# One square-root operation for two chunks of the gated recurrence in a two-layer trunk

## The chip, the cores and the metric

The kernel runs on one core of a Trainium2 chip. The metric is device time in microseconds (us) of one execution. Before the change the median of three runs is 1958.04 us (1957.45 to 1959.89). The profile shown here is of one more execution of the same program.

## What is computed

Two layers, each on 2048 rows of width 1024. A layer normalises its input, multiplies it by one wide matrix and splits the product into parts: the input `za` and gate `ga` of a linear recurrence, the latents of an attention, the attention's gate, and the input and gate of a pooling. The three results are gated, joined, multiplied by an output matrix and added to the input. The part that matters here:

```
r   = sigmoid(xa @ w_r + b_r);  i = sigmoid(xa @ w_i + b_i)      # xa = causal conv of za
log_a = -8 * r * softplus(-lam);  a = exp(log_a)
u   = sqrt(-expm1(2*log_a)) * (i * xa)
h_t = a_t * h_(t-1) + u_t                                          # along the sequence
ya  = h * silu(ga)
```

There are 384 recurrence channels (three groups `j` of 128 partitions) and the sequence is cut into four chunks `c` of 512, so a layer has 12 square roots of a 128x512 tile, and the two layers have 24.

## The kernel before, in words

The first part of each layer is a list of product groups `(m, c)`: block `m` of 128 output columns for chunk `c`. A group is 24 matmuls (L403), a little over 5 us, accumulated in one PSUM bank. The list runs over five sets of blocks (`ZSETS`): in the first three sets, for each chunk in turn, come the recurrence input `m = j` (0, 1, 2), the recurrence gate `m = 3 + j`, and two or three other blocks: the attention's gate (15, 16, 17) beside `j = 0`, pooling blocks (11, 13 and 12, 14) beside `j = 1` and `j = 2`. Weights of a block are loaded, squared, scaled and split in two halves just ahead of use: `prep` does it (DMA L216, ACT squares L222, a small matmul L228, DVE scale L185 to L190, ACT high half L231, DVE low half L232), into six slots that are reused, so later blocks can be prepared only when an earlier block has been used for the last time.

When a group's matmuls are issued, its follow-up is started as a Python generator that is stepped once or several groups later (`spawn`, `tick`). `lru_in` is the follow-up of the recurrence input: ACT takes the product out of PSUM (L474), ACT and DVE do the convolution (L476, L478), four product instructions and four tanh follow (L488, L491), then exp and tanh (L492, L493) and four DVE operations (L495 to L498) that leave in slot 1 of the chunk's scratch what the root is taken of (L496). `lru_out` is the follow-up of the gate: ACT tanh into slot 5 (L520), DVE (L521). After an odd chunk, `lru_in` issues the two roots, of the even chunk before and of its own, one after the other (L502 to L504), and then for both chunks `lru_end`: multiply (L512), the scan along the sequence (L513), a copy of its last column (L514), the gating into slot 5 (L515), and `emit_y`: a DMA of slot 5 to memory and a square with accumulation on ACT (L425, L426).

Scratch of a chunk is six slots of 128x512, chosen by `6 * (c % 2) + n`: of the eleven slots of tile `lsa`, slots 0 to 5 belong to even chunks and 6 to 10 to odd ones; the twelfth slot is in `lsb`. Slot 1 of an even chunk is `lsa[:, 1]`, that of an odd chunk `lsa[:, 7]`. The next even chunk writes slot 5 (L520) only when the even chunk before it has sent slot 5 to memory.

The source order is not the order on the engines. When the program is built, a list scheduler with a cost model of its own walks through the instructions by dependence, with source order as priority, and writes a fixed order for each engine's queue; it also places the semaphores. An instruction that becomes ready early and finds its engine free is put ahead of later ones in the source. The loads of ScalarE's function tables (ACT_TABLE_LOAD) are put in ahead of an activation that needs another set of functions than the one before it, and carry that activation's line. At run time each queue is worked through in its fixed order.

Beside this, in the same stretch, the output matrix is read and split (`out_prep`, L890 to L911, with DMAs both ways), and in the first set the next chunk's input is normalised and transposed (`hstage`: squares L340, scaling L351, transposes L356, halves L360 and L361).

Of the kernel before, what the change touches and what calls it, by code (L numbers as in the profile page):

```python
# [13 lines left out]
AF = mybir.ActivationFunctionType  # L14
# [8 lines left out]
C = 512  # L23
# [32 lines left out]
def body(nc, tc, a, ctx):  # L56
# [14 lines left out]
    def PS(tag, name):  # L71
        return psum.tile([128, 512], F32, tag=tag, bufs=BANKS[tag], name=name)
# [14 lines left out]
    tiny = cst.tile([128, 2], F32, name="tiny")  # L87
# [323 lines left out]
    def layer(st):  # L411
# [8 lines left out]
        lsa = mq.tile([128, 11, 528], F32, tag="cqh", name="lsa")  # L420
# [35 lines left out]
        def parted(x):  # L456

            xs = LT("xa", F32R)[:, 0:C], LT("xb", F32R)[:, 0:C]
            for t, h, o in ((xs[0], slice(0, 64), slice(64, 128)), (xs[1], slice(64, 128), slice(0, 64))):
                nc.scalar.activation(t[h], x[h], AF.Copy)  # L460
                nc.vector.tensor_tensor(t[o], x[h], t[h].bitcast(F32), ALU.subtract)
            return xs
# [4 lines left out]
        def scratch(c, n):  # L467
            x = 6 * (c % 2) + n
            return lsa[:, x, 0:C] if x < 11 else lsb[:, x - 11, 0:C]

        def lru_in(j, c, ps, sc):
            za, xa = lsb[:, 1 + c % 2, :], scratch(c, 0)
            nc.vector.tensor_copy(za[:, 0:3], halo[:, j, 0:3])
            nc.scalar.activation(za[:, 3 : 3 + C], ps[:], AF.Copy, scale=sc[:, 2:3])  # L474
            nc.vector.tensor_copy(halo[:, j, 0:3], za[:, C : C + 3])
            nc.scalar.activation(xa, za[:, 0:C], AF.Identity, scale=prm[:, l, j, 0:1], bias=prm[:, l, j, 4:5])  # L476
            for t in range(1, 4):
                nc.vector.scalar_tensor_tensor(  # L478
                    xa, za[:, t : t + C], prm[:, l, j, t : t + 1], xa, ALU.mult, ALU.add
                )  # L480
            xs = parted(xa)
            yield YG
            tr, ti, tt, eh = (scratch(c, n) for n in (1, 2, 3, 4))
            for b in range(2):

                pg = PS("ax", "pg")
                for i in range(2):
                    nc.tensor.matmul(pg[:], gws[j][:, i, b, :], xs[b], start=i == 0, stop=i == 1)  # L488
                for g, t_ in ((0, tr), (1, ti)):
                    h, o = slice(64 * g, 64 * g + 64), slice(64 * b, 64 * b + 64)  # L490
                    nc.scalar.activation(t_[o], pg[h, :], AF.Tanh, scale=0.5, bias=gp[h, l, j, b : b + 1])  # L491
            nc.scalar.activation(eh, tr, AF.Exp, scale=gp[:, l, j, 2:3], bias=gp[:, l, j, 2:3])  # L492
            nc.scalar.activation(tt, tr, AF.Tanh, scale=gp[:, l, j, 3:4], bias=gp[:, l, j, 3:4])  # L493

            nc.vector.scalar_tensor_tensor(eh, eh, 1.0, tt, ALU.add, ALU.mult)  # L495
            nc.vector.scalar_tensor_tensor(tr, eh, 2.0, eh, ALU.subtract, ALU.mult)  # L496
            nc.vector.tensor_scalar(tt, eh, -1.0, 1.0, ALU.mult, ALU.add)
            nc.vector.scalar_tensor_tensor(ti, ti, 1.0, xa, ALU.add, ALU.mult)  # L498
            yield 1
            if c % 2:  # L500

                for x in (c - 1, c):  # L502
                    t = scratch(x, 1)
                    nc.scalar.activation(t, t, AF.Sqrt, scale=-1.0, bias=tiny[:, 0:1])  # L504
                for x in (c - 1, c):
                    lru_end(j, x, sgs[j, x])

# [2 lines left out]
        def lru_end(j, c, sc):  # L510
            tr, ti, tt, hsn, sg = (scratch(c, n) for n in (1, 2, 3, 4, 5))
            nc.vector.scalar_tensor_tensor(ti, tr, 0.5, ti, ALU.mult, ALU.mult)  # L512
            nc.vector.tensor_tensor_scan(hsn, tt, ti, halo[:, j, 3:4], ALU.mult, ALU.add)  # L513
            nc.vector.tensor_copy(halo[:, j, 3:4], hsn[:, C - 1 : C])  # L514
            nc.vector.scalar_tensor_tensor(sg, sg, sc[:, 3:4], hsn, ALU.mult, ALU.mult)  # L515
            emit_y(sg, j, c)
# [409 lines left out]
        for g, (m, c) in enumerate(groups):  # L926
            if g < g1 and (g == 0 or (g + HL) % len(ZSETS[0]) == 0):
                nxt = (g + HL) // len(ZSETS[0]) + (1 if l == 0 else 2)
                if nxt < NC:
                    early_room = [lsb[:, 3 + n, 0:C] for n in range(4)] + [lsa[:, (7 + n) % 11, 0:C] for n in range(10)]  # L930
                    spawn(st["hstage"](nxt, True, early_room if l == 0 and nxt == 1 else None))
            for ev in events.get(g, ()):
                ev()
            for w in begin.get(g, ()):
                spawn(zweight(st, w, late=2))
            if m == "kr":
                krope()
                tick()
                continue
            ps, sc = zgroup(st, m, c, g < g1)  # L940
            if m < 3:
                spawn(lru_in(m, c, ps, sc))
            elif m < 6:
                spawn(lru_out(m - 3, c, ps, sc))
            elif m < 8:
                spawn(latent("k", m - 6, c, ps, sc))
            elif m < 11:
                spawn(latent("q", m - 8, c, ps, sc))
            elif m < 13:
                spawn(pool_in(m - 11, c, ps, sc))  # L950
            elif m < 15:
                spawn(pool_gate(m - 13, c, ps, sc))
            else:
                spawn(attn_gate(m - 15, c, ps, sc))
            tick()
# [425 lines left out]
```

## Time and profile before

| | |
|---|---|
| median of three runs | 1958.04 us |
| the profiled execution, its own time | 1964.85 us |
| its span, first to last instruction | 1962.8 us |
| mean granted TensorE clock | 0.991 |
| busy: TensorE / VectorE / ScalarE / GpSimd | 1890.9 / 1454.6 / 1145.0 / 45.5 us |
| share of the span | 96% / 74% / 58% / 2% |

PE stands for TensorE's matmuls, DVE for VectorE, ACT for ScalarE, POOL for GpSimd and SP for the engine that issues DMAs. Times inside the profile count from the start of the span. The bracket at the end of a timeline line is the time for which the engine stood idle ahead of it, and what ended the wait.

### The profile page before, as it was taken

Reading aid. Unit: us, or ns where it says so; the run is one execution under the profiler, and the core shown is the slowest. Engines: PE = TensorE matmul, PEld = TensorE weight load, DVE = VectorE, ACT = ScalarE, POOL = GpSimd, SP = SyncE. Lnnn points to the kernel's source line nnn. Section 1 sums busy time; section 2 is a strip of 40 time slices with the busy share of each in tenths; the row PEclk is TensorE's granted clock in tenths of the full one; section 3 lists DMA queues with packets and bytes.
Section 4 is the critical chain, followed back from the end, with each engine's and each line's share of the span. In section 5 each row is a group of like instructions: output and inputs, shape, how many; then the busy total and the mean of one; then the engine's idle time right before and its main releaser. Section 6 shows DMA issues by size and latency. Waiting matters only on the chain. (4 is left out here: it accounts for less than half of the span.)

```text
span 1962.8 us, 32908 instructions
## 1 busy us (share of the span) xinstructions
PE 1890.9 (96%) x12352; PEld 980.2 (50%) x12352; DVE 1454.6 (74%) x3345; ACT 1145.0 (58%) x2060; POOL 45.5 (2%) x38
## 2 busy tenths in 40 slices
PE   8999999999889999999999999999999999999998
PEld 4444444444455555555454444444444555555553
DVE  8757788767888787774485568778687977977745
ACT  8767877644355465464286578775434644644641
POOL 0000000010000000000000000001010000000000
PEclk9999999999999999999999999999999999999999
DMA  6313242212453121122751223231134621421443
GB/s 217 111 49 108 82 134 101 62 38 65 103 168 119 44 92 52 37 76 77 245 168 53 75 81 122 100 105 46 49 76 110 192 77 44 154 84 59 158 160 136
DMA packets 125280, 197.74 MB, mean 101 GB/s; under 512 B 18752, under 2 KB 41536, under 8 KB 125120
## 3 DMA queue, kind: packets, MB, share of 16 engines
q1 hardware_dynamic: 125120, 195.64, 31.6%
q8 instruction: 97, 1.59, 0.3%
q14 instruction: 63, 0.52, 0.1%
HBM read 124.59 MB, written 55.26 MB: 92 GB/s over the span
## 5 line engine op out<-in xcount | busy, mean ns | idle before, releaser
L403 PEld LDWEIGHTS <-zw 128*128 128x128 f16 x3456 | 335.9, 99 | 401.3 <-issue 22.0
L1048 ACT ACTIVATE p<-sps,tiny,sig 128x512 f32<-128x512 f32 x480 | 322.0, 710 | 326.2 <-PE sps L1045 174.7
L403 PE MATMUL zps<-hA,zw 128*128 128x512 f16 x1728 | 398.0, 384 | 5.1 <-ACT zw L231 3.9
L403 PE MATMUL zps<-hB,zw 128*128 128x512 f16 x1728 | 382.7, 379 | 0.0
L1122 PE MATMUL ops<-wo,yb 128*128 128x512 f16 x1536 | 370.2, 380 | 6.3 <-DVE xr L1114 4.0
L1049 DVE TENSOR_TENSOR pl<-p 128x1024 f16<-128x1024 f32 x240 | 253.9, 1059 | 127.2 <-ACT p L1048 101.0
L1122 PEld LDWEIGHTS <-yb 128*128 128x128 f16 x1536 | 144.9, 98 | 172.4 <-issue 9.9
L822 DVE TENSOR_REDUCE mx<-pm 128x1 f32<-128x512 f32 x288 | 192.5, 683 | 21.9 <-PE pm L817 21.8
L1043 PE MATMUL sps<-kq 97*128 97x512 f16 x480 | 167.1, 348 | 3.0 <-ACT p L1048 2.9
L1044 PE MATMUL sps<-kq 96*128 96x512 f16 x480 | 166.6, 347 | 0.0
L1045 PE MATMUL sps<-kq 96*128 96x512 f16 x480 | 165.7, 345 | 0.0
L817 PE MATMUL pm<-kq 96*128 96x512 f16 (+3 forms) x496 | 151.0, 345 | 5.6 <-DVE mx L822 2.7
L1062 PE MATMUL av<-zw,p 128*128 128x129 f16 (+1 forms) x1632 | 140.2, 214 | 5.2 <-ACT ar L1012 5.2
L1062 PEld LDWEIGHTS <-p 128*128 128x128 bf16 x1632 | 108.5, 98 | 30.4 <-PE sps L1047 1.1
L824 DVE CUSTOM_DVE_ANT_0 pm<-pm,mkq 128x128 f32<-128x128 f32 (+1 forms) x208 | 101.0, 495 | 12.7 <-PE pm L817 11.8
L1062 PE MATMUL av<-zw,pl 128*128 128x65 f16 x1632 | 92.9, 194 | 1.7 <-DVE pl L1049 1.7
L1062 PEld LDWEIGHTS <-pl 128*128 128x128 f16 x1632 | 75.1, 98 | 12.2 <-DVE pl L1049 8.0
L491 ACT ACTIVATE lsa<-pg,gp 64x512 f32<-64x512 f32 x96 | 65.3, 680 | 12.0 <-PE pg L488 10.4
L1045 PEld LDWEIGHTS <-kq 96*128 96x128 f16 x480 | 47.0, 98 | 43.6 <-issue 1.9
L1043 PEld LDWEIGHTS <-kq 97*128 97x128 f16 x480 | 46.6, 97 | 44.3 <-issue 4.7
L1044 PEld LDWEIGHTS <-kq 96*128 96x128 f16 x480 | 47.2, 98 | 43.1 <-issue 4.8
L1067 PE MATMUL av<-zw,p 128*128 128x64 f16 x336 | 64.8, 193 | 0.0
(300 smaller groups left out, 2604.1 us busy)
## 6 DMA issues: line engine op xcount, KB each, us to landing
xk<-x SPq DMA_DIRECT2D x80, 256.0 KB
raw<-win SPq DMA_DIRECT2D x72, 256.0 KB
raw<-wout SPq DMA_DIRECT2D x64, 256.0 KB
yr<-y SPq DMA_DIRECT2D x64, 256.0 KB
xr<-x SPq DMA_DIRECT2D x56, 256.0 KB
x<-xr SPq DMA_DIRECT2D x56, 256.0 KB
sg<-sg SPq DMA_DIRECT2D x48, 256.0 KB
kq<-pq SPq DMA_DIRECT2D x96, 128.0 KB
```

What stands on the lines that cost most here:

```text
L403: nc.tensor.matmul(ps[:], w[:, i, k, :], st["h"](j, k, c), start=n == 0, stop=n == 3 * KD - 1)
L491: nc.scalar.activation(t_[o], pg[h, :], AF.Tanh, scale=0.5, bias=gp[h, l, j, b : b + 1])
L817: nc.tensor.matmul(pm[:, 0:n], t[0:96, h, 2, q0 : q0 + 128], t[0:96, h, 0, s * C : s * C + n], start=True, stop=True)
L822: nc.vector.tensor_reduce(m, pm[:], AX.X, ALU.max)
L824: nc.vector.tensor_tensor_reduce(out=pm[:, 0:n], in0=pm[:, 0:n], in1=mkq[:, C - n : C], op0=ALU.add, op1=ALU.max, scale=1.0, scalar=-3.0e3 ...
L1043: nc.tensor.matmul(ps[:, o:C], t[0:97, h, 0, ks], t[0:97, h, 2, qs], start=True, stop=False)
L1044: nc.tensor.matmul(ps[:, o:C], t[0:96, h, 0, ks], t[0:96, h, 3, qs], start=False, stop=False)
L1045: nc.tensor.matmul(ps[:, o:C], t[0:96, h, 1, ks], t[0:96, h, 2, qs], start=False, stop=not diag)
L1048: nc.scalar.activation(pw_[:, h, o:C], ps[:, o:C], AF.Exp, scale=sig[:, 4:5], bias=tiny[:, 1:2])
L1049: nc.vector.tensor_tensor(pl[:, :, o:C], pw_[:, :, o:C], ph[:, :, o:C], ALU.subtract)
L1062: nc.tensor.matmul(acc[h][:, c - 64 * lo : c + 65], w, v[:, 64 - 64 * lo : QB], start=first and n == 0 and j == 0, stop=end and n == 1 and ...
L1122: nc.tensor.matmul(ps[:], yb[:, j, k, 128 * (n // 2) : 128 * (n // 2) + 128], wo[n % 2, k][:, i, :], start=m == 0, stop=m == 3 * KD - 1,)
```

## The change

The two roots after an odd chunk become one activation over both chunks' slot 1, a view of `lsa` with a step of six slots. All else is as it was.

```diff
@@ -499,9 +499,8 @@
             yield 1
             if c % 2:
 
-                for x in (c - 1, c):
-                    t = scratch(x, 1)
-                    nc.scalar.activation(t, t, AF.Sqrt, scale=-1.0, bias=tiny[:, 0:1])
+                t = lsa[:, 1:8:6, 0:C]
+                nc.scalar.activation(t, t, AF.Sqrt, scale=-1.0, bias=tiny[:, 0:1])
                 for x in (c - 1, c):
                     lru_end(j, x, sgs[j, x])
```

## Rows read from the trace of the kernel before

**Rows 1.** The page, busy time (us), share of the span, instructions of an engine

```profile
PE 1890.9 (96%) x12352; PEld 980.2 (50%) x12352; DVE 1454.6 (74%) x3345; ACT 1145.0 (58%) x2060; POOL 45.5 (2%) x38
```

**Rows 2.** Windows, six stretches with the recurrence (30 to 360, 1000 to 1320): busy us, summed

```profile
sum 650.00, PE 634.54 PEld 306.31 DVE 472.43 ACT 495.17 POOL 7.71; mean PE 105.76 PEld 51.05 DVE 78.74 ACT 82.53 POOL 1.28
```

**Rows 3.** Line 504 of the kernel: duration ns min/median/max, starts, forms

```profile
L504 ACT ACT_TABLE_LOAD  x24: 1283/1283/1283, 57.5 to 1313.0; - x24
L504 ACT ACTIVATE lsa<-lsa,tiny x24: 721/722/723, 58.8 to 1314.3; 128x512 f32<-128x512 f32 x24
```

**Rows 4.** ACT groups by line and shape: busy us, mean ns, idle before

```profile
L1048 ACT ACTIVATE p<-sps,tiny,sig 128x512 f32<-128x512 f32 x336 | 247.6, 774 | 213.1 <-PE sps L1045 174.7 <-PE sps L1047 33.2 <-DVE pl L1049 3.1
...
L520 ACT ACT_TABLE_LOAD x18 | 23.1, 1283 | 0.3
...
L1048 ACT ACTIVATE p<-sps,tiny,sig 128x128 f32<-128x128 f32 x48 | 19.9, 454 | 37.7 <-PE sps L1047 21.9 <-PE av L1062 10.7 <-DVE ysc L190 3.7
...
L715 ACT ACT_TABLE_LOAD x4 | 5.1, 1283 | 0.1
...
L1048 ACT ACT_TABLE_LOAD x2 | 2.6, 1283 | 0.0
```

**Rows 5.** ACT in order of time (start us, us), around the first chunk's root

```profile
57.54 1.28 ACT L504 ACT_TABLE_LOAD   x1
58.84 0.72 ACT L504 ACTIVATE lsa<-lsa,tiny 128x512 f32<-128x512 f32 x1
...
67.20 1.28 ACT L520 ACT_TABLE_LOAD   x1
```

**Rows 6.** PE in order of time, the longest wait of the first layer's stretches

```profile
259.30 0.61 PE L403 MATMUL zps<-hA,zw 128*128 128x512 f16 x2 [1.92 <-ACT zw L231]
```

**Rows 7.** Windows, 260 to 265: us; busy PE, PEld, DVE, ACT, POOL; granted clock; DMA

```profile
260.00:265.00 5.00, 4.71 (x14) 1.82 (x15) 4.74 (x9) 2.99 (x6) 0.00 (x0) 0.66 0.30 105
```

**Rows 8.** ACT in order of time, ahead of the wait at 259

```profile
254.00 0.72 ACT L907 ACTIVATE wp<-raw,wosc 128x512 f16<-128x512 f32 x1 [3.11 <-DMA wo<-wp]
254.74 1.28 ACT L520 ACT_TABLE_LOAD   x1
256.03 0.69 ACT L520 ACTIVATE lsa<-zps,zsc 128x512 f32<-128x512 f32 x1
...
258.54 1.32 ACT L231 ACTIVATE zw<-raw,zsc 128x512 f16<-128x512 f32 x2
```

**Rows 9.** DVE groups by line, the recurrence's end: busy us, mean ns, idle before

```profile
L513 DVE TENSOR_TENSOR_SCAN lsa<-lsa,halo 128x512 f32<-128x512 f32 x24 | 31.2, 1299 | 0.4
...
L512 DVE SCALAR_TENSOR_TENSOR lsa<-lsa 128x512 f32<-128x512 f32 x24 | 16.5, 688 | 5.0 <-ACT lsa L504 5.0
...
L515 DVE SCALAR_TENSOR_TENSOR lsa<-lsa,zsc 128x512 f32<-128x512 f32 x12 | 8.9, 742 | 0.0
...
L514 DVE COPY halo<-lsa 128x1 f32<-128x1 f32 x24 | 3.6, 149 | 0.2
```

**Rows 10.** DVE in order of time, ahead of the wait at 259

```profile
253.49 0.74 DVE L515 SCALAR_TENSOR_TENSOR lsb<-lsb,zsc,lsa 128x512 f32<-128x512 f32 x1
...
254.82 0.16 DVE L190 TENSOR_SCALAR zsc<-hb 128x2 int32<-128x2 int32 x1
```

**Rows 11.** SP in order of time, DMAs issued ahead of the wait at 259

```profile
249.56 1.10 SPq L911 DMA_DIRECT2D wo<-wp  x2
```

**Rows 12.** PE and ACT in order of time, the wait at 341, behind an even chunk

```profile
341.65 0.50 PE L572 MATMUL pg<-xh,pw 128*128 128x512 f32 x1 [0.88 <-ACT xh L567]
...
340.97 0.63 ACT L567 ACTIVATE xh<-sa 128x512 fp32r<-128x512 f32 x1 [1.22 <-DVE sa L565]
```

**Rows 13.** DVE in order of time, the even chunk's end ahead of the wait at 341

```profile
331.76 0.74 DVE L515 SCALAR_TENSOR_TENSOR lsa<-lsa,zsc 128x512 f32<-128x512 f32 x1
```

**Rows 14.** PE and ACT in order of time, the wait at 106, behind an odd chunk

```profile
106.41 0.41 PE L356 MATMUL ht<-idt,xk 128*128 128x128 f32 x2 [1.50 <-DVE xk L351]
...
93.81 0.63 ACT L426 ACTIVATE junk<-lsb 128x512 bf16<-128x512 f32 x1 [0.92 <-DVE lsb L515]
```

## The prediction, made before the changed kernel was run

> **What bounds the kernel now.** I read the page's busy times first. TensorE is busy for 1890.9 of 1962.8 us, ScalarE for 1145.0 [rows 1]: the matmuls set the time, and work taken from ScalarE counts only where TensorE waits for it. So I next summed the windows of the six stretches in which the recurrence runs. In their 650 us TensorE is busy for 634.54, which leaves 15.5 us of idle time in both layers together, while ScalarE is busy for 495.17, or 76% [rows 2]. 15.5 us is the most that the edit could take out of waits there, however much it saves on ScalarE.
>
> Then line 504 itself. The source has the two roots side by side, so one would expect one table load for a pair. The trace shows 24 loads of 1283 ns at L504, one for each of the 24 roots [rows 3], and 24 loads at the activations that follow and need the other set: 18 at L520, 4 at L715, 2 at L1048 [rows 4]. In order of time the first root runs at 58.84, alone, behind its load at 57.54, and the set is loaded back at 67.20 [rows 5]; two roots side by side would need no load between them, so each of the 24 stands alone. The list scheduler has taken the even chunk's root, and with it that chunk's scan and output, ahead of the odd chunk. One operation over both buffers can't be split that way, so what the edit really does is to tie the even chunk's end to the odd chunk's.
>
> **The change part by part.**
>
> *Table loads.* 12 roots in place of 24, with the tanh and exp of the next chunks still between them, need 12 loads and 12 loads back. Removed: 24 x 1.283 = 30.8 us of ScalarE. The sqrt of rows 5 starts 1.30 us after its load's start, so the row shows no cost beside the load's own 1283 ns. The Trainium skill, in "ScalarE: Activation LUTs", section "What ACT_TABLE_LOAD costs", puts a drain of about 1380 ns beside each load, 2.66 us in all; by that estimate the relief would be 63.8 us. The row disagrees, and the relief lies beside the matmuls in either case; the larger figure would only give more weight to the faster rival below.
>
> *The roots.* 24 x 722 ns = 17.3 us [rows 3] become 12 of twice the size. The trace has no activation of 1024 elements; the exponentials cost (774 - 454) / 384 = 0.833 ns for an element more [rows 4], so one takes 722 + 512 x 0.833 = 1149 ns, and 12 take 13.8 us. The bounds are 722 ns (a free second half) and 1444 (two roots). Removed: 3.5 us. Together ScalarE gives up 34.3 of its 1145.0 us, 3.0%. What hides all of it is the matmul stream, and without that cover it would be 34.3 us.
>
> *What is moved.* The even chunk's L512, L513, L514 and L515, 0.688 + 1.299 + 0.149 + 0.742 = 2.88 us of DVE [rows 9], its y DMA on SP and its square on ACT go later by about a chunk's time, five groups of matmuls, behind the odd chunk's root, which itself ends 0.43 us later. Twelve places (the even chunks) lose this work and twelve (the odd ones) get it twice. No one misses the even y, which is read again only by the output product at the layer's end. The state passed along the scans keeps its order. The even slot 5 is held longer, and that is the new wait: L520 of the chunk after the pair must not write it until the pair's first y has gone out. So I went through the waits of TensorE in the recurrence's stretches and asked on which side each lies.
>
> *Behind an even chunk* there is one wait of note, at 341.65, 0.88 us for L567 on ACT, which waited 1.22 us for DVE's L565 [rows 12]. The even chunk's end is part of DVE's work ahead of it: its L515 is at 331.76 and writes `lsa`, the even buffer [rows 13]. Taking 2.88 us out there covers the wait: -0.9. The second layer repeats the pattern, so twice: -1.8 us, between 0 and -1.8.
>
> *Behind an odd chunk* lies the longest: 1.92 us at 259.30, for the high half of a weight block, L231 [rows 6], and the second layer has it again at the same place. After the first the granted clock is 0.66 over five us, between the two levels 0.5 and 1 (1.2 and 2.4 GHz), behind an engine that had just stood idle [rows 7]: another 5 x 0.34 = 1.7 us. So this place costs about 3.6 us a layer, 7.2 in all. It keeps its loads, because the chunk that has just ended is an odd one, whose L515 at 253.49 writes `lsb` [rows 10]: ACT then waits 3.11 us for a DMA (L907), loads back at 254.74, does L520 at 256.03 and comes to L231 at 258.54 [rows 8]. DVE's scale for that block, L190, is done at 254.98 [rows 10], 3.6 us before L231 starts. The extra DVE work, 2.88 + 0.43 = 3.3 us, just fits into that. But slot 5's release does not: the even y now has the place of the odd one, L515 ending at 254.23 [rows 10], and a DMA of the same size, issued at 249.56 to 250.66 [rows 11], let L907 go at 254.00, 3.3 us after the issue. So L520 could start at 254.3 + 3.3 = 257.6, and not at 256.03. If the queue keeps its order, L231 is 1.6 us later in each layer, +3.2 us; if the scheduler puts L231 ahead of L520, 0 or a gain. I take half, +1.6, because the scheduler also counts DMAs, though by its own durations.
>
> At 106.41 TensorE waited 1.50 us for an input chunk whose squares stand behind the odd chunk's L426 at 93.81 [rows 14]. One more such square is 0.63 us, and waiting for both scans costs at most 2.88. I take +0.4, nearer to the square, because the squares of the input don't depend on the scans and can be put ahead. This is in the first layer alone.
>
> *Sum.* -1.8 + 1.6 + 0.4 = +0.2 us. Bounds: all of the losses and no gain, 3.2 + 2.88 = +6.1; all gains and no loss, -1.8, and -9.0 if the weight wait also goes. The profiled execution took 1964.85 us, its span and 2.05 us around it, 0.35% above the median of the runs shown; that difference is no part of the change, so I carry the sum to the median: 1958.04 + 0.2, which is **1958.2 us**. A measurement of this kernel can tell some 0.2% from no change, 3.9 us, so this is "no difference".
>
> **The rivals.**
>
> *Faster: the weight wait disappears.* A table load and reload fewer in each second chunk, and fewer DVE operations ahead, let the scheduler or the queue bring L231 forward. For it: 7.2 us hang on one ACT instruction in each layer that had its scale ready 3.6 us early [rows 8, 10]; ACT was held by L907 and not by work. Against it: the root at that place is an odd chunk's, whose two loads remain. Time: 1958.0 - 7.2 - 1.8 = 1949. I give 0.27 for over 3.9 us faster; some of the way there (one layer, or the clock alone) is enough.
>
> *Slower: the even buffer holds up ACT.* At the first L520 behind a pair, ACT, which works through its queue in order, waits for the y DMA with L231 behind it. Five pairs of six in a layer have such an L520; it decides where the next weight block has under 1.6 us to spare, which is the place at 259 [rows 6] and its like in the second layer. If both scans also stand ahead of L190, L231 comes 3.3 us later and the clock stays low for as much longer: up to 3.3 + 1.7 = 5.0 us a layer, +10 in two, less the 1.8 gained elsewhere: 1962 to 1966. For it: the 3.3 us that a DMA took here. Against it: behind the other pairs TensorE waits for no weights now, and the scheduler can fill in other work. Of the same kind is a rule of the Trainium skill, "Perfetto Trace Analysis", section "Optimizing Scalar/DVE Operations": where these engines are not saturated but cause bubbles elsewhere, smaller instructions let work be done sooner, so a merger would cost. At 76% ScalarE is such an engine. No row shows yet that a root's size holds anyone up. I give 0.26.
>
> *The edit does not do what it says.* If the merged root still saw two loads and two halves, or if the view with a step of six were taken as everything between slots 1 and 7, more waits would follow. The accesses to the slots in between come before the root or after the chain that needs it anyway, so the price would be under 1 us, and the time 1958. It lies inside "no difference", at 0.05 of its 0.47.
>
> **How the numbers follow.** No difference 0.47, faster 0.27, slower 0.26. For eight times in ten the range leaves out the far end of each rival: it goes down to 1949.5, just short of the loss of both weight waits, and up to 1965.0, one us below the full price of the slower one. The likeliest case alone spans 1954.3 to 1962.1.
>
> **What would show it.** Right: 12 roots of about 1.15 us at L504, 12 loads there and 12 at the lines behind, ScalarE's busy time near 1111 us, two sets of L512 to L515 behind each root, and TensorE's idle time in the stretches still near 15 us. The wait at 341 gone, and the start of L520 behind a pair on the landing of the pair's first y. Wrong, on the fast side: no wait for L231 and a granted clock of 1.00 in its place; on the slow side: that wait above 3 us, or new waits for weights behind other odd chunks. I would be wholly wrong if the roots were still apart in the trace, or if TensorE's busy time itself changed by more than 4 us.

## The result, and the profile after

The changed kernel is slower, by three quarters of a per cent:

| | before | after |
|---|---|---|
| median, 6 runs each (us) | 1958.97 (1954.21 to 1964.08) | 1973.15 (1971.36 to 1984.23) |
| ratio, 95% interval | | 1.0075 [1.0059, 1.0092] |
| the profiled execution, its own time (us) | 1964.85 | 1971.64 |
| its span (us), granted clock | 1962.8, 0.991 | 1969.8, 0.993 |

The two profiled executions are 6.8 us apart and the medians 14.2: the one of before is 5.9 us above its median, the one of after among its fastest. The profile therefore shows about half of the loss. From L504 on, line numbers of after are one less than before's.

The edit did what it says. From the page of after, and from the root's line and the groups of table loads:

```profile
PE 1888.2 (96%) x12352; PEld 979.8 (50%) x12352; DVE 1452.8 (74%) x3345; ACT 1110.3 (56%) x2024; POOL 47.0 (2%) x38
```

```profile
L503 ACT ACT_TABLE_LOAD  x12: 1283/1283/1283, 88.8 to 1322.0; - x12
L503 ACT ACTIVATE lsa<-lsa,tiny x12: 1147/1148/1150, 90.3 to 1323.3; 128x1024 f32<-128x1024 f32 x12
```

```profile
L519 ACT ACT_TABLE_LOAD x8 | 10.3, 1283 | 0.7 <-DMA y<-lsa 0.5
...
L714 ACT ACT_TABLE_LOAD x2 | 2.6, 1283 | 0.0
...
L1047 ACT ACT_TABLE_LOAD x2 | 2.6, 1283 | 0.0
```

Twelve roots of 1148 ns, 12 loads for them and 12 back: against [rows 3, 4], 24 loads and 34.7 us of ScalarE are gone. Nothing of that reached the end. The windows of the six stretches, summed as in [rows 2]:

```profile
sum 650.00, PE 628.65 PEld 304.43 DVE 467.98 ACT 456.27 POOL 8.64; mean PE 104.78 PEld 50.74 DVE 78.00 ACT 76.05 POOL 1.44
```

ScalarE is busy for 38.9 us less there, 4.2 more than it lost in all, because the windows stand still and the slower kernel has a little less of its work inside them. TensorE stands idle in them for 650 - 628.65 = 21.4 us instead of 15.5. Which waits grew is in the sums of TensorE's waits by the line that ended them (us in total, times, longest). First the kernel before, then after:

```profile
PE zps L403 <- ACT zw L231: 3.9, 2, 2.0
...
PE pn L245 <- DVE zsc L185: 2.8, 2, 1.4
...
PE pg L572 <- ACT xh L567: 1.8, 2, 0.9
...
PE pp L228 <- DVE wosc L185: 1.7, 2, 0.9
...
PE zps L403 <- DVE zw L232: 0.8, 2, 0.4
```

```profile
PE pp L228 <- DVE wosc L185: 5.7, 2, 2.8
...
PE pn L245 <- DVE zsc L185: 5.1, 2, 3.1
...
PE zps L403 <- DVE zw L232: 2.9, 2, 1.6
...
PE pg L571 <- ACT lsa L491: 2.8, 2, 1.5
...
PE pg L571 <- ACT xh L566: 2.3, 2, 1.7
```

Each is there twice, once in a layer. The wait for ScalarE's high half L231 is gone (-3.9) and one for DVE's low half L232 has come (+2.1). Three waits that are not for a weight block's halves grew: for DVE to read a small product out of its bank, `wosc` (+4.0) and `pn` (+2.3), and for the pooling's product at L571 (+3.3). These five make +7.8 us. All of TensorE's waits together went from 58.5 to 67.5 us, +9.0, while its busy time fell by 2.7 [rows 1]; the span grew by 7.0.

**The place at 259**, where the prediction had looked hardest. PE, ACT and DVE of after in order of time; [rows 6, 8, 10] are the same place before (L190 is the weight block's scale, L511 and L512 of after are the end's multiply and scan):

```profile
261.84 5.24 PE L403 MATMUL zps<-hA,zw 128*128 128x512 f16 x22 [1.59 <-DVE zw L232]
...
251.13 1.28 ACT L503 ACT_TABLE_LOAD   x1
252.43 1.15 ACT L503 ACTIVATE lsa<-lsa,tiny 128x1024 f32<-128x1024 f32 x1
...
254.19 1.32 ACT L231 ACTIVATE zw<-raw,zsc 128x512 f16<-128x512 f32 x2
...
262.55 1.28 ACT L519 ACT_TABLE_LOAD   x1
...
253.24 0.17 DVE L190 TENSOR_SCALAR zsc<-hb 128x2 int32<-128x2 int32 x1
253.61 1.93 DVE L511 SCALAR_TENSOR_TENSOR lsa<-lsa 128x512 f32<-128x512 f32 x2 [0.20 <-ACT lsa L503]
...
256.12 1.27 DVE L512 TENSOR_TENSOR_SCAN lsa<-lsa,halo 128x512 f32<-128x512 f32 x1
...
258.54 0.73 DVE L514 SCALAR_TENSOR_TENSOR lsa<-lsa,zsc 128x512 f32<-128x512 f32 x1
...
259.87 1.27 DVE L512 TENSOR_TENSOR_SCAN lsa<-lsa,halo 128x512 f32<-128x512 f32 x1
261.06 0.72 DVE L232 SCALAR_TENSOR_TENSOR zw<-raw,zsc,zw 128x512 f16<-128x512 f32 x1
```

ScalarE makes the high half at 254.19, 4.3 us earlier than before, ahead of the reload and of L519, so the wait in [rows 6] could not recur. But DVE now has both chunks' ends in one place. Between the scale (L190, 253.24) and the low half (L232, 261.06) stand two L511, two scans and an L514: 1.93 + 1.27 + 0.73 + 1.27 = 5.2 us. Before, L232 started at 259.49 with none of them behind the scale. The block needs both halves, and the later one decides. Even so TensorE waits less here than before: 1.59 us for L232 in place of 1.92 for L231 and 0.38 for L232 behind it. The loss lies at other places.

**The place at 230**, behind an even chunk, where DVE was relieved. PE and DVE in order of time, before and then after:

```profile
230.15 0.38 PE L228 MATMUL pp<-ssq,on 128*128 128x2 f32 x2 [0.86 <-DVE wosc L185]
...
228.61 0.74 DVE L515 SCALAR_TENSOR_TENSOR lsa<-lsa,zsc 128x512 f32<-128x512 f32 x1
...
229.94 0.16 DVE L185 TENSOR_REDUCE wosc<-pp 128x1 f32<-128x16 f32 x1
```

```profile
232.16 0.38 PE L228 MATMUL pp<-ssq,on 128*128 128x2 f32 x2 [2.85 <-DVE wosc L185]
...
230.27 0.68 DVE L461 TENSOR_TENSOR xa<-lsa,xa 64x512 fp32r<-64x512 f32 x1
230.97 0.69 DVE L461 TENSOR_TENSOR xb<-lsa,xb 64x512 fp32r<-64x512 f32 x1
...
231.94 0.17 DVE L185 TENSOR_REDUCE wosc<-pp 128x1 f32<-128x16 f32 x1
```

The even chunk's end has left this place, and yet L185 comes 2.0 us later: the fixed order now has both L461 ahead of it, which before came after it, at 232.20 and 232.92. So at this place the wait comes from a queue that was written anew, and not from work that moved into it.

### The profile page after: what moved, and what is told of

It is laid out like the page before. It is cut to its first block, busy times and chain, and to the rows that moved or that the text cites. A ratio compares the mean times of both kernels' runs of the same rounds, so it can differ in the third digit from the quotient of the medians.

```text
span 1969.8 us, 32890 instructions
## 1 busy us (share of the span) xinstructions
PE 1888.2 (96%) x12352; PEld 979.8 (50%) x12352; DVE 1452.8 (74%) x3345; ACT 1110.3 (56%) x2024; POOL 47.0 (2%) x38
## 3 DMA queue, kind: packets, MB, share of 16 engines
q8 instruction: 97, 1.59, 0.3%
## 5 line engine op out<-in xcount | busy, mean ns | idle before, releaser
L403 PE MATMUL zps<-hA,zw 128*128 128x512 f16 x1728 | 393.6, 381 | 3.3 <-DVE zw L232 2.9
L823 DVE CUSTOM_DVE_ANT_0 pm<-pm,mkq 128x128 f32<-128x128 f32 (+1 forms) x208 | 101.0, 495 | 12.6 <-PE pm L816 11.8
L491 ACT ACTIVATE lsa<-pg,gp 64x512 f32<-64x512 f32 x96 | 65.2, 679 | 4.8 <-PE pg L488 3.2
```

The source lines that it names most:

```text
L403: nc.tensor.matmul(ps[:], w[:, i, k, :], st["h"](j, k, c), start=n == 0, stop=n == 3 * KD - 1)
L823: nc.vector.tensor_tensor_reduce(out=pm[:, 0:n], in0=pm[:, 0:n], in1=mkq[:, C - n : C], op0=ALU.add, op1=ALU.max, scale=1.0, scalar=-3.0e3 ...
```

## The experiments

Theory 1 of the expectations is that the tie makes the loss: the even chunk's end must wait for the odd chunk, the two ends come in a row on DVE, and what stands behind them is late. The rival is named in each. Theory 5 is that any edit makes the scheduler write other queues, and that these happen to be worse. Idle is 650 us less TensorE's busy time in the six stretches, from one profiled execution each; the clock is the mean over the timed executions (before, in the same batches, 0.994).

| run | roots, loads | the two ends | ratio to before, 95% | idle (us) | clock |
|---|---|---|---|---|---|
| before | 24, 48 | as the scheduler likes | 1 | 15.5 | 0.994 |
| after | 12, 24 | tied | 1.0075 [1.0059, 1.0092] | 21.4 | 0.990 |
| e9_change_again | 12, 24 | tied | 1.0084 [1.0068, 1.0101] | 21.1 | 0.988 |
| e1_tied | 24, in pairs but for one, 26 | tied | 1.0108 [1.0093, 1.0124] | 25.7 | 0.990 |
| e11_tie_no_loads | 12 tanh, none | tied | 1.0086 [1.0072, 1.0101] | 20.9 | 0.988 |
| e13_ends_tied | 24, 48 | tied | 1.0062 [1.0048, 1.0076] | 20.3 | 0.990 |
| e2_bank_after | 12, 24 | tied, bank moved | 1.0056 [1.0043, 1.0069] | 17.7 | 0.990 |
| e8_later_bank | 12, 24 | tied, later, bank moved | 1.0047 [1.0033, 1.0061] | 18.9 | 0.991 |
| e5_tie_and_loads | 12 and 12 dummies, 48 | tied | 1.0034 [1.0022, 1.0046] | 18.6 | 0.992 |
| e4_no_loads | 24 tanh, none | free | 1.0054 [1.0040, 1.0068] | 21.5 | 0.991 |
| e12_each_bank | 24, 48 | written out by hand, bank moved | 1.0032 [1.0017, 1.0047] | 19.3 | 0.992 |
| e6_even_tanh | 12 and 12 tanh, 24 | free | 1.0012 [1.0003, 1.0020] | 16.9 | 0.993 |
| e14_apart_two | 12, 24 | two groups apart | 1.0013 [1.0005, 1.0022] | 15.2 | 0.992 |
| e7_apart_bank | 12, 24 | one group apart, bank moved | 1.0014 [1.0004, 1.0024] | 16.4 | 0.993 |
| e10_apart | 12, 24 | one group apart | 1.0003 [0.9995, 1.0012] | 14.9 | 0.993 |
| e3_bank_before | 24, 48 | free, bank moved | 0.9999 [0.9988, 1.0011] | 15.3 | 0.994 |

**The operation or the tie?** The kernel before with its two roots, both made to wait for the odd chunk by their bias operand, which is the same 1e-30 computed out of an odd value:

```diff
-                for x in (c - 1, c):
-                    t = scratch(x, 1)
-                    nc.scalar.activation(t, t, AF.Sqrt, scale=-1.0, bias=tiny[:, 0:1])
+                tied = small("tied", 1, bufs=2)
+                nc.vector.tensor_scalar(tied[:], scratch(c, 1)[:, 0:1], 0.0, 1e-30, ALU.mult, ALU.add)
+                for t in (scratch(c - 1, 1), scratch(c, 1)):
+                    nc.scalar.activation(t, t, AF.Sqrt, scale=-1.0, bias=tied[:, 0:1])
```

> Two roots as before, one operation for each chunk, but the even chunk's root takes its bias from a value that the odd chunk's last DVE step has made, so it can't run ahead. If the cost lies in tying the even chunk's end to the odd chunk's (theory 1), this is as slow as the change: 1967 to 1980 us, ratio to before 1.004 to 1.011, with 12 loads at the root's line. If it lies in the size of the merged operation or in its being one instruction (theory 2), this is as fast as before: 1955 to 1963 us, ratio within 0.998 to 1.002.

Measured: 1978.67 us, slower still than the change, as theory 1 has it. The loss needs no merged operation: two tied roots of 722 ns lose as well. TensorE's largest wait here is again for L231:

```profile
PE zps L403 <- ACT zw L231: 8.8, 4, 4.5
```

**The bank of the small products.** `wosc` waits because out_prep's small product and a weight block's (L228) share one PSUM buffer. Moving the first to another one, in the changed kernel and in the one before:

```diff
-            ps = PS("sm", "pp")
+            ps = PS("ax", "pp")
             nc.tensor.matmul(ps[:, 0:16], ones, ssq[:], start=True, stop=True)
```

> The changed kernel, with the small product of the output weights' scale in one of the two ax banks in place of the only sm bank. Theory 1a: the new waits of TensorE for the scale of the output weights (2.85 us in each layer, 0.9 before) come from that single bank and make part of the loss, with the clock that falls behind them: 4 to 7 us faster than the change, 1966 to 1969 us, and no wait at L228 for wosc above 0.5 us. If those waits only stand in for another that would come anyway (theory 3), the wait moves to the next weight or pooling product and the time stays at 1970 to 1976.

> The kernel before with the same bank moved. Theory 1a: it gains only the 0.9 us a layer that this wait had there, 1956 to 1959 us, ratio 0.998 to 1.000. Theory 3: no gain, 1.000. Both say that it is within 0.2% of before, so that the bank alone does not explain a difference between the two kernels unless the change makes the wait longer.

Measured: 1969.90 and 1958.05 us, the first between its two forecasts. The `wosc` wait goes, and some 3 of the 14 us come back, though the interval overlaps that of the change; the rest moved to other waits. TensorE and DVE of the changed kernel with the bank moved, in order of time:

```profile
260.24 4.00 PE L403 MATMUL zps<-hA,zw 128*128 128x512 f16 x10 [4.41 <-DVE zw L232]
...
258.27 1.27 DVE L513 TENSOR_TENSOR_SCAN lsa<-lsa,halo 128x512 f32<-128x512 f32 x1
259.46 0.72 DVE L232 SCALAR_TENSOR_TENSOR zw<-raw,zsc,zw 128x512 f16<-128x512 f32 x1
```

Without the earlier wait TensorE gets to the weight block sooner and waits 4.41 us there, for the L232 behind the second scan. In the unchanged kernel the same move is worth nothing.

**Is the relief of ScalarE worth anything?** Four kernels vary the loads. e4_no_loads and e6_even_tanh leave the tie out and take a tanh in place of the root, in all chunks or in the even ones, so u and all that follows have other values and the loads go. e11_tie_no_loads does the same to the merged operation. e5_tie_and_loads is the change with the loads put back, by a root of 512 constants into a scratch tile in each even chunk:

```diff
-                    nc.scalar.activation(t, t, AF.Sqrt, scale=-1.0, bias=tiny[:, 0:1])
+                    nc.scalar.activation(t, t, AF.Tanh, scale=-1.0, bias=tiny[:, 0:1])
```

```diff
-            if c % 2:
-
+            if not c % 2:
+                nc.scalar.activation(junk[:].rearrange("p (a b) -> p a b", a=4), ones.unsqueeze(1).broadcast_to([128, 4, 128]), AF.Sqrt, bias=tiny[:, 0:1])
+            else:
```

> The kernel before with tanh in place of the root (other values come out): two operations, no tie, and no table loads at all but the first, 61 us less of ScalarE. If ScalarE is off the path (theory 1), 1952 to 1962 us, ratio 0.997 to 1.002. If ScalarE's time counts in this stretch (theory 4), at least a third of the matmul waits there goes, and the clock dips with them: 1945 to 1951 us, ratio under 0.996.

> The kernel before with tanh for the even chunks' roots alone (other values come out): no tie, 24 loads as in the changed kernel, half of the relief of ScalarE. Theory 1: the tie is all, so 1957 to 1962 us, ratio 0.998 to 1.002. Theory 4 turned round: half of the run without loads, 1962 to 1967 us, ratio 1.002 to 1.004. Theory 5 (any rewriting of the queues loses some of what this order happened to have, the more the further it goes): 1960 to 1968 us with the waits at other places than in the run without loads.

> The changed kernel with a root of 512 constants in each even chunk, where the even chunk's own root stood: its two loads and its time on ScalarE are back (48 loads), the even chunk's end stays tied to the odd one's. If the loss comes from the lighter ScalarE, for which the queues are written closer together (theory 4, turned round by the run without loads), the time comes back to 1957 to 1964 us. If it comes from the tie, which puts two chunks' ends on DVE at once (theory 1), it stays at 1969 to 1980 us.

> The changed kernel with tanh in the merged operation (other values come out): the tie, and no loads. If the two parts that the earlier runs separate add up (tie 0.34% with all loads in place, relief of ScalarE 0.54% without a tie): ratio 1.007 to 1.011, 1973 to 1982 us. If less work on ScalarE helps once the tie is there: under 1.006, below 1970 us.

Measured: 1968.57, 1962.05, 1965.53 and 1977.22 us. The prediction took the relief to be worth nothing, and in no run here was it worth more. Without a tie, the kernel with all loads gone is slower by 0.54%, outside both forecasts; with half of them gone the difference of 0.12% is too small to decide anything. With the tie, putting 24 back takes away about half of the loss, between the two forecasts, but taking the last 24 out changes nothing (e11_tie_no_loads 1.0086, e9_change_again 1.0084, in the same batch). From the waits of e4_no_loads:

```profile
PE pg L572 <- ACT lsa L491: 7.1, 3, 3.8
PE pp L228 <- DVE wosc L185: 6.0, 2, 3.0
```

No chunk waits for another there, ScalarE has 59 us less to do in the stretches, and TensorE waits longer for the same small products. So theory 1 can't be the whole of it. What is left is theory 5, that any edit here also makes the scheduler write another order of the queues, and that these orders were worse; that is argued from the trace, and not isolated.

**Ends apart.** The merged root stays, the odd chunk's end follows one product group after the even one's, or two:

```diff
-                for x in (c - 1, c):
-                    lru_end(j, x, sgs[j, x])
+                lru_end(j, c - 1, sgs[j, c - 1])
+                yield 1
+                lru_end(j, c, sgs[j, c])
```

It was run first with the bank moved (e7_apart_bank), then by itself beside a repetition of the change, and with `yield 2` (e14_apart_two).

> The changed kernel with the bank of the second run, and the odd chunk's end one product group (5 us) later than the even one's. If two ends in a row on DVE, ahead of the low half of a weight block, make the wait of 4.41 us at 260 (theory 1), that wait falls under 2 us and the time to 1960 to 1967 us. If any rewriting costs (theory 5), new waits come elsewhere and the time is 1966 to 1976 us.

> The changed kernel with the odd chunk's end one product group later than the even one's, and no other bank. Theory 1 (two ends in a row on DVE are the cost): 1963 to 1969 us, ratio 1.002 to 1.005, the wait for the output weights' scale still there at 2 to 3 us a layer. If the bank alone had made the seventh run good: 1968 to 1976 us, as the change.

> The changed kernel once more, beside the other three on one chip. 1970 to 1976 us, ratio 1.006 to 1.009, if the first measurement holds; under 1.005 if two of its six executions, at 1979.65 and 1984.23, had made it what it was.

> The change with the odd chunk's end two product groups after the even chunk's (one in the run that came back to the time before). Theory 1: the loss stays away, ratio 0.998 to 1.002; if more distance also takes the remaining wait for wosc (4.6 us) down, 0.996 to 0.999. Rival (one group was a lucky order of the queues): ratio over 1.003.

Measured: 1962.11, 1960.17, 1976.44 and 1961.91 us. One group of distance gives back 16 us, and two do the same to within 0.1%. DVE of e10_apart at the place at 259, and TensorE there:

```profile
255.66 1.28 DVE L512 TENSOR_TENSOR_SCAN lsa<-lsa,halo 128x512 f32<-128x512 f32 x1
...
258.89 2.55 DVE L232 SCALAR_TENSOR_TENSOR zw<-raw,zsc,zw 128x512 f16<-128x512 f32 x2
...
262.91 1.28 DVE L512 TENSOR_TENSOR_SCAN lsa<-lsa,halo 128x512 f32<-128x512 f32 x1
...
255.75 10.09 PE L403 MATMUL zps<-hA,zw 128*128 128x512 f16 x46
```

The second scan stands behind L232 now, L232 starts 2.2 us earlier than in after, and TensorE runs through 46 matmuls without a wait. Its waits for the lines of above, in e10_apart:

```profile
PE pp L228 <- DVE wosc L185: 4.6, 2, 2.3
...
PE pn L245 <- DVE zsc L185: 3.1, 2, 1.6
```

The weight waits are gone, both kinds (4.7 us in the kernel before), and `pn` is nearly back at its 2.8 us. `wosc` keeps most of what it grew by, and all waits at L571 are 4.3 us (2.3 before, 5.5 in after). Gains and losses about cancel: all of TensorE's waits are 57.6 us here, 58.5 before, so this version only draws level with the kernel before. None of the versions beat it by more than a measurement can tell.

**Another place for the whole pair.** One more `yield 1` ahead of the merged root, bank moved (the next even chunk's gate then overwrites slot 5, so `ya` has other values):

> The changed kernel with the bank of the second run, and the merged root and both ends one product group later. Theory 1: the pair of ends then stands behind the weight block that it delayed, but still in one piece: the wait at 260 goes and one of 1 to 3 us may come behind it, 1963 to 1970 us. Theory 5: 1966 to 1976 us. If the root's lateness itself were the cost (theory 2), it is slower than the second run by over 2 us.

Measured: 1968.50 us, no different from e2_bank_after by the intervals, and inside the bands of theories 1 and 5 both. Moving the pair of ends by one group did not help; TensorE's longest waits are now for the pooling's `xh`, 7.0 us in two.

**The order of the trace before, written out in the source.** Root and end right behind each chunk, bank moved:

```diff
-            if c % 2:
-                t = lsa[:, 1:8:6, 0:C]
-                nc.scalar.activation(t, t, AF.Sqrt, scale=-1.0, bias=tiny[:, 0:1])
-                for x in (c - 1, c):
-                    lru_end(j, x, sgs[j, x])
+            t = scratch(c, 1)
+            nc.scalar.activation(t, t, AF.Sqrt, scale=-1.0, bias=tiny[:, 0:1])
+            lru_end(j, c, sgs[j, c])
```

> Root and end written out after each chunk, odd or even, with the bank of the third run: the source then says what the trace of the kernel before shows, 48 loads and no tie. If that order is what makes the kernel before fast: 1954 to 1961 us, ratio 0.997 to 1.001. If the source order alone, with the same dependences, writes other queues and loses something (theory 5): 1962 to 1970 us.

Measured: 1967.49 us. This takes no work away and ties nothing, and still loses 0.3%, as theory 5 has it. Source order is the scheduler's priority, and here it alone was changed, beside a bank that by itself costs nothing (e3_bank_before).

**The pair of ends alone.** The last question was whether two ends in a row make a loss with everything else as before: two roots, free to run ahead, and all 48 loads. Only the 0.5 of L512 comes out of an odd value (twelve DVE operations of 0.147 us):

```diff
+                half = small("half", 1, bufs=2)
+                nc.vector.tensor_scalar(half[:], scratch(c, 1)[:, 0:1], 0.0, 0.5, ALU.mult, ALU.add)
...
-            nc.vector.scalar_tensor_tensor(ti, tr, 0.5, ti, ALU.mult, ALU.mult)
+            nc.vector.scalar_tensor_tensor(ti, tr, half, ti, ALU.mult, ALU.mult)
```

> The kernel before with its two roots and 48 loads, roots free to run ahead, but the 0.5 that both ends multiply by comes out of a value of the odd chunk, so that the two chunks' ends come in a row on DVE behind the odd chunk as in the changed kernel. Theory 1 (the loss is two ends in a row, 2 x 2.88 us of DVE work in one place): slower, ratio 1.003 to 1.008, with a wait of zps for zw of over 2 us behind odd chunks. Rival (the loss needs the later even root or the fewer loads, whose absence reshuffles the queues): ratio 0.999 to 1.002, and zps waits as before, 3.9 us in all.

Measured: 1971.99 us, 1.0062, inside the band of theory 1. The weight wait is there, 2.13 us long in the first layer, but it was 1.92 in the kernel before, so it says little; `pn`, `wosc` and the wait at the pooling's product grew, as in after. Its sums of TensorE's waits, and its groups of loads:

```profile
PE pn L245 <- DVE zsc L185: 5.5, 2, 3.2
...
PE zps L403 <- ACT zw L231: 4.3, 2, 2.1
...
PE pp L228 <- DVE wosc L185: 3.7, 2, 2.4
...
PE pg L574 <- ACT lsa L491: 3.0, 2, 1.6
```

```profile
L506 ACT ACT_TABLE_LOAD x24 | 30.8, 1283 | 0.4
...
L522 ACT ACT_TABLE_LOAD x20 | 25.7, 1283 | 7.4 <-DMA y<-lsa 7.2
```

All 24 loads for the roots are there, each root alone, and the loss is nearly the change's. The even chunk's late end also holds up ScalarE here, which waits 7.2 us for the DMA of slot 5 (0.5 in after), so this run does not tell the two ends in a row from the even end being late.

**What is settled and what is open.** Tying the even chunk's end to the odd one is enough for a loss (e13_ends_tied, e1_tied), and putting the two ends a group apart in the changed kernel takes it away, with the merged root and the saved loads kept (e10_apart against e9_change_again, in the same batch). With the ends apart, the merged root and the saved loads together cost and gain nothing that a measurement can tell. The tie is not needed for a loss: e4_no_loads and e12_each_bank lose without one. Open is how much of each difference is the tie and how much the new order that came with it, which of the scheduler's decisions makes each new wait, at 230 above all, and why less ScalarE work gave a worse order in e4_no_loads: no run held the order of the queues fixed.

## Why the prediction was wrong

**Right.** It saw that the two roots ran apart, that the edit really ties the even end to the odd chunk, and that TensorE is the bound and the relief lies beside the matmuls. Root (1149 forecast, 1148 ns measured), loads and ScalarE's busy time (1111, 1110.3 us) came as worked out. The first layer's wait for a normalised input grew by 0.55 us, where 0.4 was taken, though all waits at L356 in both layers together hardly changed (10.3 and 10.4 us):

```profile
109.50 0.41 PE L356 MATMUL ht<-idt,xk 128*128 128x128 f32 x2 [2.05 <-DVE xk L351]
```

**The step that failed** is the one behind the sum: "So I went through the waits of TensorE in the recurrence's stretches and asked on which side each lies." It priced the waits at three places, 341, 259 and 106, with each queue otherwise as it was, and put all else at nothing, because "behind the other pairs TensorE waits for no weights now, and the scheduler can fill in other work". In the profiles, two layers together, 259 was charged +1.6 us and came to -1.8 (L231 -3.9, L232 +2.1); 341 was charged -1.8 and came to +3.3; and `wosc` (+4.0) and `pn` (+2.3), which had no term, made up most of the loss. The reading "one wait of note" behind an even chunk was wrong too: the 0.86 us for `wosc` at 230 were there, as long as the 0.88 at 341 and also behind an even chunk's end on DVE. By the prediction's own reasoning that wait should have shrunk, and it grew by 2.0 us in each layer.

**The overlap at 259** failed as well: "The extra DVE work, 2.88 + 0.43 = 3.3 us, just fits into that." It measured the slack of one instruction, the scale L190, whose work on ScalarE was late at the time, and put the extra work into it. But the block also waits for DVE's low half, and that had nothing in hand: in the kernel before TensorE's next matmuls waited for it too. PE in order of time, the line behind [rows 6]:

```profile
260.29 6.61 PE L403 MATMUL zps<-hA,zw 128*128 128x512 f16 x22 [0.38 <-DVE zw L232]
```

In place of a fit the runs show L232 1.57 us later, at 261.06, and a wait of 1.59 us for it, 4.41 where the `wosc` wait ahead of it is taken away, and none where one scan is put behind it.

**The wrong queue.** The price of +1.6 for L520 waiting for slot 5's y did not come: L231 had been put ahead of L519, and ScalarE stood idle for that DMA for only 0.5 us in the whole kernel. The mechanism is real, 7.2 us of such idle time in e13_ends_tied, but it isn't the one that made the change slower. The slower rival had the right sign (0.26) with this price; something like its aside, "If both scans also stand ahead", happened, but ahead of L232 and not of L190. The faster rival's own event, L231 brought forward, took place and took 3.9 us of waits away; what the rival left out was DVE, where 2.1 came back, and all other places.

**The sign of a gain.** "Taking 2.88 us out there covers the wait: -0.9." At 341 the wait for the pooling's product did not vanish, it grew from 0.88 [rows 12] to 1.48 us, with a ScalarE tanh as its releaser. PE and ACT in order of time, the ACT line of before last:

```profile
343.89 0.50 PE L571 MATMUL pg<-xh,pw 128*128 128x512 f32 x1 [1.48 <-ACT lsa L491]
...
341.35 0.63 ACT L566 ACTIVATE xh<-sa 128x512 fp32r<-128x512 f32 x1 [3.93 <-DVE sa L564]
...
343.15 2.10 ACT L491 ACTIVATE lsa<-pg,gp 64x512 f32<-64x512 f32 x3
```

```profile
338.38 1.36 ACT L491 ACTIVATE lsa<-pg,gp 64x512 f32<-64x512 f32 x2
```

The relief of DVE did come: DVE's last step for the pooling, L564, started at 340.56, 0.4 us later than before, where TensorE ran 1.6 us later. But the order on ScalarE was new. It stood idle for 3.93 us for L564, with all four L491 behind, two of which ran ahead of that step before; TensorE needs their bank.

The prediction moved work within queues that it otherwise took as fixed. It priced one possible reordering, of L231 and L520, and no others. Of the +9.6 us of `wosc`, `pn` and L571, the traces show a new order at 230 and at 341. At `pn` they show the same DVE operations in the same order, only later: L185 reads that bank at 386.06 and not at 382.58, 3.5 us later, where TensorE's product ahead of the wait (L228) came 1.8 us later.

```profile
386.06 0.15 DVE L185 TENSOR_REDUCE zsc<-pp 128x1 f32<-128x2 f32 x1
```

That place lies outside the six stretches, behind the last pair of ends, and with the ends apart its growth is nearly gone. The prediction's bounds were worked out from its three places alone, and so the range ended at 1965.0.

**The clock, at one place of many.** It charged low clock behind one wait, [rows 7]. In after that place runs at 1.00 behind its shorter wait, and the clock falls elsewhere: 0.83 from 1245 to 1255 us in the profile, behind a wait of 1.69 us at L571. Over the timed executions the mean clock is 0.990 in after against 0.994 for the kernel before in the other batches. By a rough estimate from these, 0.004 x 1960 = 8 us of the 14.2 go with the lower clock, beside the length of the waits; no run changed the clock by itself, so that the waits lowered it is not shown. The profile, with a clock of 0.993 against 0.991, has none of this part.

**The Trainium skill's rule** from "Perfetto Trace Analysis", section "Optimizing Scalar/DVE Operations", that smaller instructions may let work be done sooner, came out with the right sign for another reason: two small roots that wait for the odd chunk lose no less than the merged one (1.0108 and 1.0075), and the merged one loses nothing once the ends are apart (1.0003). No run here shows a price of the size itself.

## What to carry to other kernels

Merging operations of two tiles ties the earlier tile's whole tail to the later one, so price the tail and not the operation alone, and ask what two tails in a row stand ahead of on the engine that runs them; if something there is due, put the second tail a step later. When a block needs halves from two engines, read the slack of both: a wait that names one engine says nothing about the other. Where a scheduler fixes the queues at build time, taking work off an engine that isn't the bound has no sure sign. Look at every wait of the bounding engine, not only the longest, and leave a forecast of "hidden, so free" room on the slow side until the new order is known: here edits cost up to 0.5% without a tie and up to 1.1% with one.

## What the runs showed of the hardware

An activation over two 128x512 buffers, six slots apart, takes 1148 ns where two take 2 x 722: the second half costs 426 ns, which is 0.832 ns for an element. At this place a table load delayed nothing beyond its own 1283 ns: at 252.43 the merged root starts 1.30 us after its load, as the small one did in [rows 5]. This disagrees with the drain of about 1380 ns that the Trainium skill puts beside each load ("ScalarE: Activation LUTs", "What ACT_TABLE_LOAD costs").

An execution's time roughly follows its granted clock. Of the six of the changed kernel one took 1971.64 us at 0.993 and the slowest 1984.23 at 0.985, 12.6 us for 0.008, where the clock in full proportion would make 0.008 x 1970 = 15.8; only roughly, because the fastest, 1971.36, had 0.990. In the table of the runs the kernels with more idle time mostly have the lower mean clock, 0.994 at 15 us and 0.988 at 21, though e1_tied has 0.990 at 25.7. So one profile of each kernel, taken at about the same clock, understated what the change costs.
